# The first mixer's output product as seven half-size products, with the memory's norm and transposes moved to that mixer's start

## The chip, the cores and the metric

One core of a Trainium2 chip. The time is device microseconds of one execution of the whole program, the median of several; beside it one execution was taken with the hardware profiler.

## The reference

Two residual layers over 512 tokens of width 1024, each with a mixer, a cross-attention into 256 memory tokens and a feed-forward part. What matters here is the mixer of layer 0 and the memory's keys and values:

```python
for layer in range(DEPTH):
    h = rmsnorm(x, g_mix_pre[layer])
    # layer 0: forgetting attention (y_a) and short convolution (y_b)
    y = concatenate([y_a, y_b], axis=-1) @ w_out      # 512x1024 @ 1024x1024
    x = x + rmsnorm(y, g_mix_post[layer])
    h = rmsnorm(x, g_cross_pre[layer])
    m = rmsnorm(mem, g_mem[layer])
    y = memory_cross_attention(h, m, w_q, w_kv, w_o)
    ...
```

In the attention the cumulative log of a forget gate (`cum`, from log_sigmoid and a running sum over the tokens) is added to the scores.

## The kernel before

All products run on TensorE as three products of split operands: an operand is a high part (rounded to the matmul's input type, made on ScalarE) and a low part (what is left, made on VectorE), and high x high, high x low and low x high are added up in PSUM. `split_out` (L527) makes both parts; `split_w` does it for a weight tile of 128x1024 that SP has loaded (`st`): `wh` by ScalarE, `wl` by VectorE. PSUM has two families of banks, `bA` and `bB`, taken in turn by `bankA()` and `bankB()`.

Layer 0's mixer is `fox`. It makes v for the attention, the forget gate, then q and k of head pairs 0 and 1 (`qk_pairs(0)`), and then `weave` runs two generators against each other on TensorE: `main` (the convolution's and attention's projections, `conv(0)`, `qk_pairs(2)`, `conv(2)`, then the first column half of the output product) and `side` (the attention of the four head pairs). The forget gate's chain is: `z`, `log1p` (a row of dependent instructions of 8x512 on VectorE), a scan over the tokens, a DMA from GpSimd that writes the sums to `cum`, and a broadcast of `cum` back as `cb` for the first softmax steps (the custom instruction on L1386).

The output product is an `OutProj`: `half0_steps` computes columns 0 to 511 for four row tiles over 8 contraction tiles (in steps of `main`, as operands come), `half1` columns 512 to 1023 row tile by row tile. Each row tile's end is followed by `chain` (sum of squares, gain, addition to x), `next` (the norm of the following sub-layer, `h`) and `transpose` (h into `hT`, through PSUM). That makes 8 x 4 x 2 x 3 = 192 matmuls of 128x512.

The memory is loaded, normalised (`memory_rows`: two squares, a small rstd chain with the power on GpSimd, two scalings, for each of two row tiles) and transposed (`memory_T`) inside `half1` of layer 0. The transposed rows are kept in DRAM as `memT` for layer 1. Then `memory_kv` computes the keys (four chunks c of 48 matmuls of 128x256) and the values (matmuls of 128x512).

Every engine works its queue in order, and what the order is comes from the order in which the program issues, except where a hand-written order holds. SP issues weight loads; after the first loads `pace` puts DRAM copies of the feed-forward's factors behind some of them (`copies`), and `spend` issues accumulating DMAs on GpSimd (`adds`) that make sums of them.

Of the kernel before, what the change touches and what calls it, by code (L numbers as in the profile page):

```python
# [15 lines left out]
P = 128  # L16
# [26 lines left out]
def trunk_kernel(ctx: ExitStack, tc: tile.TileContext, a: dict, out: bass.AP):  # L43
# [103 lines left out]
    def spend(n, behind=None):  # L147
# [16 lines left out]
        ("gp", a["g_mix_pre"][1].rearrange("(m p) -> m p", p=P)),  # L164
    )
# [153 lines left out]
    def put_T_pair(hT, hss, j, gain):  # L319
# [8 lines left out]
        for k, v in ks:  # L328
            nc.scalar.mul(out=hT.hi[k][:, 0:256], in_=v, mul=ch(gain, k))
        for k, v in ks:  # L330
            nc.vector.scalar_tensor_tensor(out=hT.lo[k][:, 0:256], in0=v, scalar=ch(gain, k), in1=f(hT.hi[k][:, 0:256]),
                                           op0=ALU.mult, op1=ALU.subtract)
# [632 lines left out]


# [18 lines left out]
    def memory_T(layer, bank):  # L985


        raw = f(group("mTr")).rearrange("p a (b c) -> p (a b) c", c=MEM)
        ghi, glo = group("mTh"), group("mTl")
        vhi = ghi.rearrange("p a (b c) -> p (a b) c", c=MEM)  # L990
        vlo = glo.rearrange("p a (b c) -> p (a b) c", c=MEM)
        if layer:
            nc.sync.dma_start(out=raw, in_=memT)
        else:
            mg = memory_rows()

        def turn(t):
            for hf in range(2):
# [5 lines left out]
                nc.scalar.copy(out=raw[:, hf * 4:hf * 4 + 4, t * P:(t + 1) * P], in_=ps.rearrange("p (k c) -> p k c", k=4))  # L1004

# [8 lines left out]
        def last():  # L1014
            turn(1)
            nc.gpsimd.dma_start(out=memT, in_=raw)
            parts(range(KT))

        if layer:
            return vhi, vlo, (lambda: parts(range(4)), lambda: parts(range(4, KT)))  # L1020
        return vhi, vlo, (lambda: turn(0), last)

    def memory_kv(layer, vhi, vlo, between):
# [5 lines left out]
        for c in range(4):  # L1029
            ws = w_chunk(w, c * 256)  # L1030
# [8 lines left out]
        between()  # L1039
        vh, vl = group("vh"), group("vl")  # L1040
        for nh in range(2):
# [10 lines left out]
            for j in range(2):  # L1052
                split_out(banks[j], vh[:, 2 * j + nh, :], vl[:, 2 * j + nh, :])
        return kh, kl, vh, vl
# [149 lines left out]
    def fox(proj):  # L1204
# [125 lines left out]
        y = Feat([None] * KT, [None] * KT)  # L1330
        yg, qk, cs = {}, {}, {}
        done = set()
        TO = [(0, 0), (1, 0), (2, 0), (1, 384)]

        def y_group(m):
            if m not in yg:
                yg[m] = group("y")
                y.hi[m], y.lo[m] = yg[m][:, 0, :], yg[m][:, 1, :]
                y.hi[4 + m], y.lo[4 + m] = yg[m][:, 2, :], yg[m][:, 3, :]
            return yg[m]  # L1340
# [237 lines left out]
    for layer in range(2):  # L1578
# [16 lines left out]
        def rest():  # L1595
            for t in (2, 3):
                pm.transpose(t)
# [33 lines left out]
```

## Time and profile before

| | |
|---|---|
| time, median of 3 runs | 1390.54 us (1390.12 to 1390.89) |
| the profiled execution's own time | 1390.6 us |
| its span | 1388.8 us |
| mean granted TensorE clock | 0.996 |
| ScalarE busy | 725.3 us, 52% of the span |
| GpSimd busy | 111.7 us, 8% of the span |
| DMA | 233.62 MB moved, mean 168 GB/s |

The page of the profile lists the busy time of each engine, the chain of work that ended last and the costliest groups of instructions. A row of a timeline has the start and the duration in us, the engine, the line, the operation, the tiles that it writes and reads with their size, and in brackets how long the engine was idle before it and who released it. Matmuls overlap, so their pace is read from their starts. A row of the windows has, for a stretch, the length, then the busy us and the number of instructions of PE, PEld, DVE, ACT and POOL, the granted clock, the DMA share and the GB/s.

### The profile page before, as it was taken

To read this page: it belongs to the slowest core of one execution; us is meant where nothing else is said; L and a number is where in the kernel's file an instruction comes from. 1 tells how busy PE (TensorE), PEld (TensorE's weight loads), DVE (VectorE), ACT (ScalarE), POOL (GpSimd) and SP (SyncE) were. 2 spreads that over 40 slices of the span, in tenths; PEclk is the share of its full clock that TensorE was granted. 3 is DMA by queue.
4 is the path that set the end of the run, shared out by engine and by line. 5 is a ranking of instruction groups with operands and counts; after the bars stand their busy time and mean duration, and the time that the engine had idled before them with its cause. 6 is when DMAs were issued, how large, how long until landed. Compare 5 with 4: busy or idle time off the path is not lost.

```text
span 1388.8 us, 21766 instructions
## 1 busy us (share of the span) xinstructions
PE 1375.6 (99%) x8416; PEld 1225.7 (88%) x8416; DVE 1110.5 (80%) x1801; ACT 725.3 (52%) x1187; POOL 111.7 (8%) x161
## 2 busy tenths in 40 slices
PE   8999999999999999999999999999999999999997
PEld 6778788988899999998889888988889999999886
DVE  6876677646589999989898999663568999999987
ACT  4354456434465444456674797453456444445663
POOL 1000002011010101000011000101200011000001
PEclk9999999999999999999999999999999999999999
DMA  6844452667424567566665657256812555666653
GB/s 225 277 156 158 139 178 66 210 158 148 106 92 137 155 158 186 159 231 229 196 220 178 223 169 248 82 185 153 166 61 92 168 152 174 153 176 239 208 188 132
DMA packets 155250, 233.62 MB, mean 168 GB/s; under 512 B 8477, under 2 KB 90497, under 8 KB 153866
## 3 DMA queue, kind: packets, MB, share of 16 engines
q1 hardware_dynamic: 134706, 180.25, 40.1%
q0 software_dynamic: 17072, 46.16, 15.2%
q10 hardware_dynamic: 3368, 5.82, 1.3%
q8 instruction: 66, 1.08, 0.3%
q14 instruction: 38, 0.31, 0.1%
HBM read 219.60 MB, written 58.74 MB: 200 GB/s over the span
## 4 chain that ended last, share of the span: by engine, by line
PE 98%; DMA 1%; issue 1%; DVE 0%; POOL 0%; SPq 0%; ACT 0%; DVEq 0%; POOLq 0%
PE bA L336 14%; PE bA L338 14%; PE bA L337 14%; PE bB L336 6%; PE bB L337 6%; PE bB L338 6%; PE bB L810 3%; PE bB L812 3%; PE bB L811 3%; PE bA L810 2%; PE bA L812 2%; PE bA L811 2%; PE bA L569 2%; PE bA L571 2%; PE bB L571 2%; PE bB L569 2%
## 5 line engine op out<-in xcount | busy, mean ns | idle before, releaser
L546 DVE TENSOR_TENSOR wl<-st,wh 128x1024 fp32r<-128x1024 f32 x108 | 131.2, 1221 | 96.2 <-ACT wh L545 94.9
L545 ACT CAST wh<-st 128x1024 fp32r<-128x1024 f32 x108 | 113.1, 1050 | 119.5 <-PE bA L337 70.2
L336 PE MATMUL bA<-hTh,wh 128*128 128x512 f32 (+1 forms) x448 | 171.4, 383 | 0.2 <-ACT hTh L314 0.2
L337 PE MATMUL bA<-hTl,wh 128*128 128x512 f32 (+1 forms) x448 | 167.8, 375 | 0.3 <-DVE hTl L315 0.3
L338 PE MATMUL bA<-hTh,wl 128*128 128x512 f32 (+1 forms) x448 | 168.1, 375 | 0.0
L437 ACT CAST wg<-wr 128x1024 fp32r<-128x1024 f32 x80 | 83.6, 1045 | 49.1 <-DVE wr L466 38.4
L776 ACT CAST wh<-st 128x1024 fp32r<-128x1024 f32 x76 | 74.9, 985 | 63.6 <-PE bA L812 27.0
L338 PEld LDWEIGHTS bA<-hTh,wl 128*128 128x128 f32 x448 | 84.3, 188 | 15.4
L438 DVE TENSOR_TENSOR wg<-wr,wg 128x1024 fp32r<-128x1024 f32 x80 | 97.1, 1214 | 0.0
L337 PEld LDWEIGHTS bA<-hTl,wh 128*128 128x128 f32 x448 | 84.6, 189 | 14.1 <-DVE hTl L315 0.5
L336 PEld LDWEIGHTS bA<-hTh,wh 128*128 128x128 f32 x448 | 84.5, 189 | 14.0 <-ACT hTh L314 0.5
L781 DVE TENSOR_TENSOR wl<-st,wh 128x1024 fp32r<-128x1024 f32 x76 | 86.1, 1133 | 10.2 <-ACT wh L776 10.2
L437 ACT CAST wh<-tt 128x1024 fp32r<-128x1024 f32 x40 | 42.1, 1053 | 61.4 <-DVE tt L466 61.4
L336 PE MATMUL bA<-hTq,wh 128*128 128x256 f32 x208 | 59.2, 284 | 0.0
L338 PE MATMUL bA<-hTq,wl 128*128 128x256 f32 x208 | 58.8, 283 | 0.0
L337 PE MATMUL bA<-hTq,wh 128*128 128x256 f32 x208 | 58.8, 283 | 0.0
L810 PE MATMUL bB<-wh,ya 128*128 128x512 f32 x148 | 57.6, 389 | 0.0
L811 PE MATMUL bB<-wl,ya 128*128 128x512 f32 x148 | 57.6, 389 | 0.0
L812 PE MATMUL bB<-wh,ya 128*128 128x512 f32 x148 | 57.6, 389 | 0.0
L756 DVE TENSOR_TENSOR ya<-yb,ya 128x512 fp32r<-128x512 f32 x84 | 53.3, 638 | 0.0
L810 PE MATMUL bA<-wh,ya 128*128 128x512 f32 x132 | 51.3, 389 | 0.0
L811 PE MATMUL bA<-wl,ya 128*128 128x512 f32 x132 | 51.3, 389 | 0.0
(375 smaller groups left out, 4428.4 us busy)
## 6 DMA issues: line engine op xcount, KB each, us to landing
wr<-in_w_ffn_gu_dram SPq DMA_DIRECT2D x80, 512.0 KB
st<-t SPq DMA_DIRECT2D x40, 512.0 KB
t<-in_w_ffn_down_dram SPq DMA_DIRECT2D x32, 512.0 KB
st<-in_w_xkv_dram SPq DMA_DIRECT2D x32, 512.0 KB
st<-in_w_ffn_down_dram SPq DMA_DIRECT2D x30, 512.0 KB
st<-in_ab_w_in_dram SPq DMA_DIRECT2D x24, 512.0 KB
y<-yr POOLq DMA_DIRECT2D x18, 512.0 KB, 3.9
t<-in_w_ffn_down_dram POOLq DMA_DIRECT2D x16, 512.0 KB, 8.7
```

The lines of the kernel that those rows point to most:

```text
L336: nc.tensor.matmul(out=ps, lhsT=wh, rhs=xh, start=first, stop=False)
L337: nc.tensor.matmul(out=ps, lhsT=wh, rhs=xl, start=False, stop=False)
L338: nc.tensor.matmul(out=ps, lhsT=wl, rhs=xh, start=False, stop=last)
L437: return (lambda: nc.scalar.copy(out=to[0], in_=src), lambda: nc.vector.tensor_tensor(out=to[1], in0=src, in1=f(to[0]), op=ALU.subtract))
L438: lambda: nc.vector.tensor_tensor(out=to[1], in0=src, in1=f(to[0]), op=ALU.subtract))
L545: nc.scalar.copy(out=hi, in_=src)
L546: nc.vector.tensor_tensor(out=lo, in0=src, in1=f(hi), op=ALU.subtract)
L776: nc.scalar.copy(out=self.wt[s][0], in_=self.st[s])
L781: nc.vector.tensor_tensor(out=lo, in0=self.st[s], in1=f(hi), op=ALU.subtract)
L810: nc.tensor.matmul(out=banks[t], lhsT=yh, rhs=wh[:, jj, :], start=first and jj == 0, stop=False)
L811: nc.tensor.matmul(out=banks[t], lhsT=yh, rhs=wl[:, jj, :], start=False, stop=False)
L812: nc.tensor.matmul(out=banks[t], lhsT=yl, rhs=wh[:, jj, :], start=False, stop=last and jj == n - 1)
```

## The change

The output product of layer 0's mixer becomes a `MixProj`. With the tokens and the features cut in two, and the columns of the weight too, the product is a 2x2 block product. Its eight block products are replaced by seven (Strassen's scheme in Winograd's form), on sums and differences of blocks. Factors `t1` to `t4` are sums of weight blocks, made in DRAM by a copy and an accumulating DMA each half. Factors `n3`, `s2`, `n1` and `n4` are differences of operand blocks, made in place by VectorE and split there. Each product is two pieces j of 12 matmuls of 128x512 with their own weight tile; the results are combined on VectorE (14 instructions of 128x512).

The memory's rows are loaded and normalised right after `qk_pairs(0)`, and transposed in `main` after `conv(0)`. Both layers read the transposed rows back from `memT`. In layer 0 the gain of the next norm is applied at the transposes' end (`put_T_pair`, with the gain from a table of channels), and h is scaled on ScalarE. The steps behind the product (`tail`) run between the chunks of `memory_kv`.

```diff
+    class MixProj(DownProj):
+        PIECES = tuple((n, j) for n in ("a11", "n3") for j in range(2)) + tuple(
+            (n, j) for j in range(2) for n in ("a22", "a12")) + tuple((n, j) for n in ("s2", "n1", "n4") for j in range(2))
+        B = {"a11": "b11", "n3": "t3", "a22": "t4", "a12": "b21", "s2": "t2", "n1": "t1", "n4": "b22"}
+        SUMS = {"n3": ("a21", "a11"), "s2": ("a22", "n3"), "n1": ("a11", "s2"), "n4": ("a12", "s2")}
...
+        def plan(self):
+            for to, frm, add in (("t3", "b12", "b22"), ("t2", "b11", "t3"), ("t4", "b21", "t2"), ("t1", "b11", "b12")):
+                for js in ((0, 2), (2, 4)):
+                    copies.append(lambda to=to, frm=frm, js=js: nc.sync.dma_start(
+                        out=self.rows(to, *js), in_=self.rows(frm, *js)))
+                    adds.append(lambda to=to, add=add, js=js: nc.gpsimd.dma_start(
+                        out=self.rows(to, *js), in_=self.rows(add, *js), accum_op=ALU.add))
...
+        def sub(self, o, js=slice(0, 4)):
+            x_, y_ = self.SUMS[o]
+            nc.vector.tensor_tensor(out=self.operand(o, js), in0=self.operand(x_, js), in1=self.operand(y_, js), op=ALU.subtract)
...
+        def first_pair(self, j):
+            js = slice(2 * j, 2 * j + 2)
+            self.sub("n3", js)
+            self.split("a11", js)
+            self.split("n3", js)
...
+        def piece(self, s):
+            name, j = self.PIECES[s]
+            self.need(s + 2)
...
+            for kk in range(2):
+                k = 2 * j + kk
+                for t in range(2):
+                    ts = slice(t * P, t * P + P)
+                    bk = self.bk[name][t]
+                    nc.tensor.matmul(out=bk, lhsT=hi[:, k, ts], rhs=wh[:, kk, :], start=k == 0, stop=False)
+                    nc.tensor.matmul(out=bk, lhsT=hi[:, k, ts], rhs=wl[:, kk, :], start=False, stop=False)
+                    nc.tensor.matmul(out=bk, lhsT=lo[:, k, ts], rhs=wh[:, kk, :], start=False, stop=k == 3)
+                    yield 1
...
+        def finish(self, ahead):
+            self.run(8, 9)
+            for o in ("n1", "n4"):
+                self.sub(o)
+                self.split(o)
+            self.need(12)
+            for t in two:
+                tt(self.q[t], bk["s2"][t], self.p1[t], ALU.subtract)
+            self.run(10, 11)
+            for t in two:
+                tt(self.v[t], self.v[t], self.q[t], ALU.add)
+                tt(self.c21[t], bk["a22"][t], self.v[t], ALU.subtract)
+                self.square(t, 0, self.c21[t])
+            for t in two:
+                tt(self.p1[t], bk["a12"][t], self.p1[t], ALU.add)
+                self.square(2 + t, 0, self.p1[t])
+            ws = ahead()
+            for t in two:
+                tt(self.q[t], bk["n1"][t], self.q[t], ALU.add)
+                tt(self.v[t], bk["n1"][t], self.v[t], ALU.add)
+                self.square(t, 1, self.v[t])
+            self.run(12, 13)
+            return ws
...
             def put_b(banks):
                 for i in range(2):
-                    c = cs[m0 + i]
-                    nc.vector.tensor_tensor(out=c, in0=c, in1=banks[i], op=ALU.mult)
-                    gy = y_group(m0 + i)
-                    split_out(c, gy[:, 2, :], gy[:, 3, :])
+                    nc.vector.tensor_tensor(out=proj.act(0, m0 + i), in0=cs[m0 + i], in1=banks[i], op=ALU.mult)
+                proj.first_pair(m0 // 2)
...
         def main():
             yield from conv(0)
+            yield from memory_turn(mg, bankA)
             yield from qk_pairs(2)
             yield from conv(2)
-            yield from proj.half0_steps((4, 6), True, False)
+            yield from proj.piece(0)
+            yield from proj.piece(1)
+            proj.keep("a11")
+            yield from proj.piece(2)
+            yield from proj.piece(3)
+            proj.keep("n3")
             yield lambda: ("y", 1) in done
-            yield from proj.half0_steps((0,), False, False)
+            for m in range(2):
+                proj.split2(m)
+            yield from proj.piece(4)
+            yield from proj.piece(5)
...
         for _ in qk_pairs(0):
             pass
-        proj.y = y
+        mg = memory_rows()
         weave(main(), side())
```

Where the rows stand now is decided by the order of issue. On VectorE around the forget gate's scan, there stood before (`e`, `t` and `z` are the gate's tiles, `qk` a split of q or k):

```order
L188 SCALAR_TENSOR_TENSOR e<-e,t_456 8x512
L1323 MEMSET t_455 8x512
L1320 SCALAR_TENSOR_TENSOR z<-z,e 8x512
L546 TENSOR_TENSOR wl<-st,wh 128x1024
L1324 SCALAR_TENSOR_TENSOR e<-t_455,z 8x512
L546 TENSOR_TENSOR qk<-bA,qk 128x512
L546 TENSOR_TENSOR wl<-st,wh 128x1024
```

And now on VectorE at the same place, where `mem` is the memory's rows (128x512) or their small row statistics (128x1):

```order
L225 TENSOR_SCALAR mem<-mem 128x1
L185 SCALAR_TENSOR_TENSOR e<-e,t_460 8x512
L229 SCALAR_TENSOR_TENSOR mem<-mem 128x1
L185 SCALAR_TENSOR_TENSOR e<-e,t_460 8x512
L1158 TENSOR_SCALAR mem<-mem 128x512
L189 SCALAR_TENSOR_TENSOR e<-e,t_461 8x512
L1497 MEMSET t_460 8x512
L1494 SCALAR_TENSOR_TENSOR z<-z,e 8x512
L1158 TENSOR_SCALAR mem<-mem 128x512
L1498 SCALAR_TENSOR_TENSOR e<-t_460,z 8x512
L547 TENSOR_TENSOR qk<-bA,qk 128x512
```

Four instructions of the memory's norm stand in the gate's chain ahead of the scan (L1498), and the weight split that stood there comes after it.

On ScalarE at the end of `conv(0)`, there stood before (`y` is a split of the convolution's output, `p` a softmax step, `wh` a weight's high part, `pT` the split of a transposed softmax block):

```order
L1390 ACTIVATE p,fx<-p,fx 128x384 x2
L545 CAST y<-cs 128x512
L1390 ACTIVATE p,fx<-p,fx 128x512 x2
L545 CAST wh<-st 128x1024
L545 CAST y<-cs 128x512
```

And now on ScalarE at the same place (`yp` are the high parts of a11 and n3, `mTr` the transposed memory):

```order
L1560 ACTIVATE p,fx<-p,fx 128x384 x2
L1560 ACTIVATE p,fx<-p,fx 128x512 x2
L546 CAST wh<-st 128x1024
L546 CAST yp<-yr 128x2x256 x2
L1171 COPY mTr<-bA 128x4x128 x4
L546 CAST pT<-bB 128x512 x2
```

The four copies out of the transposes' banks stand behind two casts of the convolution's operands.

On VectorE in `memory_kv`, there stood before, for the key chunks:

```order
L631 TENSOR_TENSOR yb<-bB,gain 128x512
L634 SCALAR_TENSOR_TENSOR x_113<-ya,post,x_113 128x512
L634 SCALAR_TENSOR_TENSOR x_113<-yb,post,x_113 128x512
L224 TENSOR_SCALAR pre<-pre 128x1
L228 SCALAR_TENSOR_TENSOR pre<-pre 128x1
L258 SCALAR_TENSOR_TENSOR h<-x_113,pre,gain 128x512 x2
L546 TENSOR_TENSOR wl<-st,wh 128x1024 x2
L546 TENSOR_TENSOR kl<-bA,kh 128x512
```

And now on VectorE, from the last two combinations of the product (L1110) to just behind the first weight split of chunk c = 2 (`c_n` and `c_a` hold results of the product, `kl` the low part of keys):

```order
L1110 TENSOR_TENSOR c_a_1882<-bB,c_a_1882 128x512 x2
L547 TENSOR_TENSOR kl<-bA,kh 128x512
L822 TENSOR_TENSOR c_n_1952<-c_n_1952,gain 128x512 x2
L225 TENSOR_SCALAR post<-post 128x1
L822 TENSOR_TENSOR c_n_1952<-c_n_1952,gain 128x512
L229 SCALAR_TENSOR_TENSOR post<-post 128x1
L822 TENSOR_TENSOR c_n_1952<-c_n_1952,gain 128x512
L831 SCALAR_TENSOR_TENSOR x_110<-c_n_1952,post,x_110 128x512 x2
L225 TENSOR_SCALAR post<-post 128x1
L547 TENSOR_TENSOR wl<-st,wh 128x1024
L229 SCALAR_TENSOR_TENSOR post<-post 128x1
L547 TENSOR_TENSOR kl<-bA,kh 128x512
```

The gain products and additions to x, which stood ahead of the keys, now stand between their weight splits.

200 lines of the change are left out of this document (154 added, 46 removed).

## The prediction

> **What bounds the kernel now.** I read the page's busy times first, then its chain of waits, then TensorE's timeline and the windows around the places that the change touches.
>
> ```profile
> span 1388.8 us, 21766 instructions
> PE 1375.6 (99%) x8416; PEld 1225.7 (88%) x8416; DVE 1110.5 (80%) x1801; ACT 725.3 (52%) x1187; POOL 111.7 (8%) x161
> PE 98%; DMA 1%; issue 1%; DVE 0%; POOL 0%; SPq 0%; ACT 0%; DVEq 0%; POOLq 0%
> ```
>
> TensorE (PE) is busy for 99% of the span and carries 98% of the chain that ended last. So a matmul that is removed counts in full, and so does every pause that is put between two matmuls. The next view is the windows of the stretches that the change touches (busy us and instructions of each engine, granted clock, DMA share, GB/s).
>
> ```profile
> 40.00:60.00 20.00, 20.00 (x90) 16.09 (x89) 19.12 (x41) 6.99 (x9) 0.00 (x0) 1.00 0.98 329
> 60.00:61.00 1.00, 1.00 (x6) 0.82 (x5) 1.00 (x2) 0.00 (x0) 0.00 (x0) 1.00 1.05 403
> 62.00:63.00 1.00, 1.00 (x6) 0.84 (x5) 1.00 (x2) 0.00 (x0) 0.00 (x0) 1.00 0.28 53
> 201.00:258.00 57.00, 57.00 (x362) 51.50 (x361) 38.47 (x72) 32.46 (x69) 7.31 (x12) 1.00 0.39 120
> ```
>
> TensorE has no pause in any of them. But two neighbours are full where the change puts work: VectorE (DVE) is busy 19.12 of 20 us from 40 to 60 us, and the DMA engines 0.98 of it. From 201 to 258 us, mixer's end and memory keys, VectorE has 18.5 us free of 57.
>
> **The saving.** Start to start, from TensorE's timeline, since matmuls overlap and their durations (0.39 us) say nothing of their pace:
>
> ```profile
> 109.81 0.39 PE L336 MATMUL bA<-hTh,wh 128*128 128x512 f32 x1
> ...
> 111.62 0.39 PE L338 MATMUL bA<-hTh,wl 128*128 128x512 f32 x1
> ...
> 234.21 0.28 PE L336 MATMUL bA<-mTh,wh 128*128 128x256 f32 x1
> 234.32 0.28 PE L337 MATMUL bA<-mTl,wh 128*128 128x256 f32 x1
> ...
> 224.10 1.04 PE L305 MATMUL bA<-ident,h 128*128 128x128 f32 x8
> 224.90 0.47 PE L569 MATMUL bB<-rh,y 128*128 128x512 f32 x1
> ```
>
> The first two rows stand eight matmuls apart: 1.81 / 8 = 0.226 us for 128x512. A 128x256 takes about 0.12 (0.11 here), a 128x128 transpose 0.80 / 8 = 0.10. The output product falls from 192 matmuls of 128x512 (8 contraction tiles, 4 row tiles, 2 column halves, 3 split terms) to 7 x 24 = 168. The transposes stay at 16 of the memory and 32 of h. So 24 x 0.226 = **5.4 us** go from TensorE, and nothing else does.
>
> **The first wait: the memory's norm lands in the forget gate's chain.** The chain is VectorE's log1p and scan, a DMA of the sums (cum) to memory, its broadcast back (cb), and the first softmax step of attention(0).
>
> ```profile
> 61.57 1.21 DVE L1324 TENSOR_TENSOR_SCAN e<-t,z 8x512 f32<-8x512 f32 x1
> ...
> 72.31 0.29 DVE L1386 CUSTOM_DVE_ANT_0 p<-bB,cb 128x128 f32<-128x128 f32 x1 [5.70 <-DMA cb<-cum]
> ```
> ```profile
> 63.08 0.71 POOL L1328 DMA_DIRECT2D cum<-e  x1 [36.94 <-DVE e L1324]
> 66.99 1.13 POOL L1364 DMA_DIRECT2D cb<-cum  x2 [3.21 <-DMA cum<-e]
> ```
> ```profile
> 73.01 1.10 PE L1379 MATMUL bB<-qk 64*128 64x384 f32 x6
> ```
>
> Scan end 62.8, cum issued 63.1, cb issued 67.0, first step 72.31. The third group of score matmuls at 73.01 takes a bank which that step frees; the step with its row sum ends at 72.6, so the slack is 0.4 us. The change puts four small instructions and four scalings of the memory's norm around the scan, half of them ahead of it. They wait for four squares on ScalarE (ACT), and these for the memory's rows, which SP issues here:
>
> ```profile
> 51.62 0.56 SPq L694 DMA_DIRECT2D t<-in_w_ffn_down_dram  x1
> 56.56 0.38 SPq L119 DMA_DIRECT2D st<-in_ab_w_in_dram  x1
> 56.99 0.56 SPq L694 DMA_DIRECT2D t<-in_w_ffn_down_dram  x1
> ```
>
> The four loads stand between the first two rows' places. Traffic queued then stays dense until 61 and thins out between 61 and 63 (windows above), so what is issued near 56.9 lands near 62 to 63. The memory's 1 MB at 329 GB/s is 3.2 us more, less 1.6 us for two gain broadcasts of 0.25 MB that go. I take 60 to 62.5 for the four rows. A square takes 0.74 us start to start:
>
> ```profile
> 206.86 0.60 ACT L220 ACTIVATE junk<-bA 128x512 bf16<-128x512 f32 x1 [2.30 <-PE bA L571]
> ...
> 207.60 0.60 ACT L220 ACTIVATE junk<-bA 128x512 bf16<-128x512 f32 x1
> ```
> ```profile
> 213.01 0.88 DVE L982 TENSOR_SCALAR mem<-mem 128x512 f32<-128x512 f32 x2 [0.75 <-POOL mem L232]
> ```
>
> Two squares end near 62, the small steps and the power on GpSimd (0.75 of waiting, row above) near 63; then one scaling (0.42), the last log1p step, the memset and z (0.7 + 0.4 + 0.6), another scaling, and the scan of 1.2: its end near 66.7 in place of 62.8. Less 0.4 of slack, **+3.5 us**. Ends: rows landing 1.5 us earlier give 2; rows at 63.6 give 5.
>
> **Clock.** A pause of that length touches TensorE's clock, as the start shows (windows of 3.41 us):
>
> ```profile
> 6.87:10.28 3.41, 1.48 (x9) 0.84 (x8) 1.26 (x3) 1.37 (x2) 0.00 (x0) 1.00 1.02 402
> 10.28:13.69 3.41, 3.20 (x8) 2.44 (x9) 3.13 (x8) 2.78 (x6) 0.00 (x1) 0.50 1.05 404
> 13.69:17.10 3.41, 2.75 (x15) 1.89 (x14) 2.46 (x3) 0.83 (x2) 1.47 (x1) 1.00 1.08 353
> ```
>
> After a window with 1.48 us of PE work the next was granted 0.50; after one of 3.20 it was 1.00 again. A window at half clock full of matmuls loses 3.41 / 2 = 1.7 us. Pauses of 3.5 and 2.3 us can each leave a window with less than 1.5 us of work, if they fall well. I take **+1.5 us**; ends 0 and 3.4. The Trainium skill ("TensorE: Matmul & The Clock Gate", What's actually happening) has the clock halve after an idle window of about 3.4 us; by that rule neither pause fills a whole window except by luck and the term is nearly nothing. The trace disagrees as far as 1.48 busy of 3.41 was enough, so my term goes by the rows.
>
> **The second wait: memory transposes after conv(0).** They take four bA banks, and ScalarE's copies out of them stand behind two new casts of the convolution's operands. The second cast waits for VectorE's n3 subtraction, and this stands behind a weight split:
>
> ```profile
> 109.83 1.05 ACT L545 CAST wh<-st 128x1024 fp32r<-128x1024 f32 x1
> ...
> 214.99 1.07 ACT L1004 COPY mTr<-bA 128x512 f32<-128x512 f32 x2
> ```
> ```profile
> 111.21 1.22 DVE L546 TENSOR_TENSOR wl<-st,wh 128x1024 fp32r<-128x1024 f32 x1
> 112.35 0.68 DVE L546 TENSOR_TENSOR y<-cs,y 128x512 fp32r<-128x512 f32 x1
> ```
>
> Split end 112.35; subtraction of 128x512 to 112.95; cast to 113.5; copy (0.53) to 114.1. TensorE would be at qk_pairs(2), whose first matmul takes the first of these banks, after 16 transposes from 109.81, at 111.6 to 111.8. **+2.3 us**; ends 1.7 (casts earlier by one VectorE step) and 2.6.
>
> **The third and fourth.** Before the a22 piece ScalarE copies n3's bank out (0.5) and then casts the operand (0.6), while TensorE has the other bank's three matmuls (0.7) to do: with the handovers **+0.7**, ends 0 and 1. Then the stretch from the a22 piece to the first v matmul. TensorE has 120 matmuls of 0.226, 192 of 0.12 and 16 transposes: 27.1 + 23.0 + 1.7 = 52 us. VectorE must do in the same stretch, in this order and all of it needed by its end, 22 operations of 128x1024 (16 weight splits, 3 operand splits, 3 subtractions), 29 of 128x512 (14 combinations, 8 gain products, 7 splits), 8 additions to x, 16 of 128x256 and 14 tiny ones. The paces, start to start:
>
> ```profile
> 241.84 2.35 DVE L546 TENSOR_TENSOR wl<-st,wh 128x1024 fp32r<-128x1024 f32 x2
> 244.11 0.68 DVE L546 TENSOR_TENSOR kl<-bA,kh 128x512 fp32r<-128x512 f32 x1
> ...
> 207.58 0.69 DVE L592 TENSOR_TENSOR ya<-bA,gain 128x512 f32<-128x512 f32 x1 [1.77 <-ACT junk L220]
> 208.19 0.14 DVE L224 TENSOR_SCALAR post<-post 128x1 f32<-128x1 f32 x1
> ...
> 216.56 0.75 DVE L634 SCALAR_TENSOR_TENSOR x<-ya,post,x 128x512 f32<-128x512 f32 x1
> 217.23 0.75 DVE L634 SCALAR_TENSOR_TENSOR x<-yb,post,x 128x512 f32<-128x512 f32 x1
> 223.63 3.25 DVE L1010 SCALAR_TENSOR_TENSOR mTl<-mTr,chan,mTh 128x256 fp32r<-128x256 f32 x8
> 226.80 0.68 DVE L315 TENSOR_TENSOR hTl<-bA,hTh 128x512 fp32r<-128x512 f32 x1
> ```
>
> So 22 x 1.135 + 29 x 0.61 + 8 x 0.67 + 16 x 0.40 + 14 x 0.13 = 56.3 us, and about 1 us in which VectorE waits for ScalarE's first casts: 5 us over. It shows where memory_kv's weight splits come late (c = 2, both halves) and at the first split for v. **+5.0 us**; a pace 5% faster, or idle time that I don't see, gives 2 or 8. ScalarE's gain: eight h scalings leave VectorE, in the sum already.
>
> The weight copies and accumulating sums of the half-size factors (8 and 8 of 512 KB, on SP and GpSimd) go ahead of the FFN's and fall mostly here:
>
> ```profile
> 110.00:190.00 80.00, 80.00 (x421) 63.64 (x421) 54.06 (x121) 40.48 (x79) 1.30 (x4) 1.00 0.45 141
> ```
>
> Over half the DMA time is free there, and 16 transfers of 0.5 MB, read and written at 329 GB/s, take 50 us of it at most in place of the FFN's, which move back: I cost them at nothing, and 3 us each if one came late. The weight load behind the memory's rows on SP lands some 3 us later, but its cast stands behind the first softmax step (72.31): nothing. The memory's transposes read back cost layer 0 a load of 1 MB, some 3 us, with 10 us of pieces ahead of its use: nothing.
>
> **Sum**, against the profiled execution's own 1390.6 us (span 1388.8 and 1.8 around it; the median of the runs shown is 1390.54, so no correction): 1390.6 - 5.4 + 3.5 + 1.5 + 2.3 + 0.7 + 5.0 = **1398.2 us**, 0.55% slower. With the ends: 1390.6 - 5.4 + 2 + 0 + 1.7 + 0 + 2 = 1390.9, and 1390.6 - 5.4 + 5 + 3.4 + 2.6 + 1 + 8 = 1405.2.
>
> **Rivals.**
> - Lead covers the waits. If every operand is ready early enough that lateness is eaten by its lead, only the saving is left: 1390.6 - 5.4 = **1385.2**. It decides where leads exceed 3.5 us at the first softmax step, 2.3 at the memory's banks and 5 in the keys. For it: TensorE paused nowhere between 17 and 742 us before, and 18.5 us of VectorE are free from 201 to 258. Against it: the 0.4 us between step and score matmuls, and that the banks' copies cannot start before the transposes.
> - VectorE fits, the early waits stay: the net addition to VectorE, about 10 us by the instructions, is put into its 18.5 free us. Then 1398.2 - 5.0 = 1393.2; with the memory's rows 1.5 us earlier and no slow window, 1390.2: **no change**. For it: free time is there on average. Against it: weight splits of the pieces move behind the attention's end, seven more than before.
> - The clock halves after each pause: four pauses of 1 to 3 us in the keys leave slow windows too, 3 x 1.7 us on top: **1403**.
>
> **How the numbers follow.** A measurement of this kernel tells about 0.2% (2.8 us) from no change. My forecast has 0.52 (1393.4 to 1401), the lead 0.18, the fit 0.17, the clock 0.13. So slower 0.65, same 0.17, faster 0.18. The range that holds 8 in 10 goes from 1386.5 to 1405.2: it takes in the fit, the clock and both ends of the terms, and leaves out most of the lead.
>
> **What would show it.** TensorE pausing before the third score group of attention(0), with cb the releaser; before qk_pairs(2), with ScalarE's copy of mTr; in memory_kv before a matmul with wl, VectorE the releaser and busy throughout. 168 matmuls in the pieces at 0.226 show the saving. Slow windows show in the granted clock behind 73 and 112 us. The forecast is wrong if the memory's rows land before 57 us, or if VectorE shows idle time between the a22 piece and v.

## The result, and the profile after

| | before | after |
|---|---|---|
| time, median of 4 runs each | 1390.33 us (1390.01 to 1390.89) | 1407.15 us (1403.35 to 1409.81) |
| the profiled execution's own time | 1390.6 us | 1409.81 us |
| matmuls in the records | 8416 | 8392 |
| mean granted TensorE clock | 0.996 | 0.990 |

The change is slower: the ratio is 1.0118, its interval 1.0092 to 1.0145. The forecast was 1398.2 with a range of 1386.5 to 1405.2. The sign was right, and the loss was more than twice what was forecast: 16.8 us between the medians in place of 7.6.

The page of after: the span, the busy time of each engine, and the chain by engines.

```profile
span 1407.9 us, 21840 instructions
PE 1380.5 (98%) x8392; PEld 1227.9 (87%) x8392; DVE 1129.1 (80%) x1829; ACT 743.0 (53%) x1216; POOL 131.2 (9%) x173
PE 91%; DVE 3%; DMA 2%; issue 1%; ACT 1%; POOL 1%; SPq 0%; DVEq 0%; POOLq 0%; ACTq 0%
```

The matmuls fell by 24, exactly as the change says. Yet TensorE's busy time rose by 4.9 us in a span that is 19.1 longer: it does less work, some of it at a lower clock, and it pauses. The chain says who it waits for: VectorE, DMA, ScalarE and GpSimd hold 7% of it, against 1% before. The windows of after (length; busy us and instructions of PE, PEld, DVE, ACT, POOL; granted clock; DMA share; GB/s) show where:

```profile
72.40:75.82 3.42, 1.18 (x6) 0.61 (x4) 0.63 (x3) 0.07 (x1) 0.00 (x0) 1.00 0.82 179
75.82:79.23 3.41, 2.51 (x9) 1.67 (x10) 1.56 (x7) 1.86 (x5) 0.00 (x0) 0.50 0.79 286
79.23:82.64 3.41, 3.41 (x9) 2.32 (x7) 3.05 (x13) 1.66 (x6) 0.00 (x0) 0.50 0.40 108
116.77:120.19 3.42, 1.16 (x11) 0.91 (x10) 3.28 (x5) 2.10 (x5) 0.00 (x0) 1.00 0.21 40
120.19:123.60 3.41, 3.41 (x11) 2.73 (x12) 0.55 (x2) 1.86 (x4) 0.54 (x1) 0.50 0.99 378
249.90:253.31 3.41, 1.17 (x10) 0.96 (x9) 2.95 (x7) 1.59 (x5) 0.88 (x1) 1.00 0.00 0
253.31:256.72 3.41, 2.72 (x12) 2.64 (x12) 2.92 (x6) 2.38 (x7) 0.55 (x1) 0.50 0.39 124
256.72:260.14 3.42, 2.65 (x12) 2.44 (x12) 3.42 (x9) 0.71 (x2) 1.62 (x1) 0.50 0.45 120
260.14:263.55 3.41, 3.41 (x18) 3.41 (x17) 2.57 (x5) 0.52 (x1) 3.37 (x2) 0.50 0.44 138
270.38:273.79 3.41, 2.50 (x20) 2.18 (x19) 3.41 (x9) 3.38 (x9) 0.00 (x0) 1.00 0.00 0
273.79:277.20 3.41, 1.94 (x8) 1.61 (x9) 3.41 (x9) 2.06 (x5) 1.25 (x1) 1.00 0.19 50
201.00:258.00 57.00, 51.93 (x276) 44.53 (x275) 48.55 (x69) 38.26 (x65) 1.43 (x2) 0.96 0.68 238
210.44:272.49 62.05, 57.18 (x329) 51.19 (x329) 53.33 (x83) 41.91 (x76) 7.48 (x6) 0.92 0.58 200
```

From 201 to 258 us TensorE was busy throughout before; now it is idle for 5.1 us. The short windows are cut where the granted clock changes, which is at steps of 3.41 us. Three of them, at 72, 117 and 250 us, hold 1.2 us of work, and behind each the clock is 0.50: for two windows, one, and three. It stays at 0.50 as long as a slow window has pauses of its own (2.51, 2.72 and 2.65 us busy), and is back behind a full one. Together 20.5 us were at half clock between 20 and 1376 us; before, none of that stretch was. The last pause, at 272.5, falls on two windows (2.50 and 1.94 busy) and slows nothing.

The pauses themselves, from TensorE's timeline of after: the first and second wait.

```profile
73.13 0.40 PE L339 MATMUL bA<-hTh,wl 128*128 128x512 f32 x1
75.77 0.66 PE L1549 MATMUL bB<-qk 64*128 64x384 f32 x1 [2.24 <-DVE fx L1556]
77.33 1.32 PE L1549 MATMUL bB<-qk 64*128 64x384 f32 x5 [0.90 <-DVE fx L1556]
```
```profile
115.88 1.91 PE L1168 MATMUL bA<-ident,mem 128*128 128x128 f32 x16
120.05 0.69 PE L337 MATMUL bA<-hTh,wh 128*128 128x512 f32 x1 [2.26 <-ACT mTr L1171]
```

And three of those in memory_kv:

```profile
239.30 0.39 PE L339 MATMUL bA<-mTh,wl 128*128 128x256 f32 x1 [0.85 <-DVE wl L547]
254.00 0.58 PE L339 MATMUL bA<-mTh,wl 128*128 128x256 f32 x1 [2.93 <-DVE wl L547]
275.26 0.50 PE L1222 MATMUL bA<-wl,mTh 128*128 128x512 f32 x1 [2.38 <-DVE wl L547]
```

Counted as time between two starts beyond their usual spacing, the first wait is 2.4 + 1.4 = 3.8 us and the second 2.4. In the same way the a22 piece pauses 0.7 us at 209.5, and memory_kv 1.0 (at 238), 3.1 (251), 1.1 (256.5), 0.5 (264.5) and 2.5 (272.5), together 8.2.

### The profile page after: what moved, and what is told of

Same layout as the page of the kernel before. It is cut to its first block, busy times and chain, and to the rows that moved or that the text cites. A ratio compares the mean times of both kernels' runs of the same rounds, so it can differ in the third digit from the quotient of the medians.

```text
span 1407.9 us, 21840 instructions
## 1 busy us (share of the span) xinstructions
PE 1380.5 (98%) x8392; PEld 1227.9 (87%) x8392; DVE 1129.1 (80%) x1829; ACT 743.0 (53%) x1216; POOL 131.2 (9%) x173
## 4 chain that ended last, share of the span: by engine, by line
PE 91%; DVE 3%; DMA 2%; issue 1%; ACT 1%; POOL 1%; SPq 0%; DVEq 0%; POOLq 0%; ACTq 0%
PE bA L337 13%; PE bA L339 13%; PE bA L338 13%; PE bB L337 6%; PE bB L338 6%; PE bB L339 6%; PE bB L813 3%; PE bB L811 3%; PE bB L812 3%; PE bA L813 2%; PE bA L811 2%; PE bA L812 2%; PE bA L572 2%; PE bA L570 2%; PE bA L571 2%; PE bA L1405 1%
## 5 line engine op out<-in xcount | busy, mean ns | idle before, releaser
L547 DVE TENSOR_TENSOR wl<-st,wh 128x1024 fp32r<-128x1024 f32 x118 | 142.9, 1222 | 89.7 <-ACT wh L546 88.8
L546 ACT CAST wh<-st 128x1024 fp32r<-128x1024 f32 x118 | 123.8, 1052 | 107.3 <-PE bA L338 59.6
L777 ACT CAST wh<-st 128x1024 fp32r<-128x1024 f32 x76 | 75.0, 987 | 62.2 <-PE bA L813 26.9
L782 DVE TENSOR_TENSOR wl<-st,wh 128x1024 fp32r<-128x1024 f32 x76 | 86.7, 1141 | 10.1 <-ACT wh L777 10.1
L233 POOL TENSOR_TENSOR post<-post,nhalf 128x1 f32<-128x1 f32 x24 | 15.1, 632 | 500.4 <-DVE post L229 500.4
```

The source lines that it names most:

```text
L546: nc.scalar.copy(out=hi, in_=src)
L547: nc.vector.tensor_tensor(out=lo, in0=src, in1=f(hi), op=ALU.subtract)
L777: nc.scalar.copy(out=self.wt[s][0], in_=self.st[s])
L782: nc.vector.tensor_tensor(out=lo, in0=self.st[s], in1=f(hi), op=ALU.subtract)
```

## The experiments

Where nothing else is said, an experiment is the changed kernel with the edit shown, timed against the kernel before, whose median was 1390.3 to 1391.2 us each time. "Below the change" is against the change's median of 1407.15.

### The memory's rows and their norm behind conv(0)'s first products

```diff
+                else:
+                    rows.append(memory_rows())
...
-            yield from memory_turn(mg, bankA)
+            yield from memory_turn(rows[0], bankA)
...
-        mg = memory_rows()
         weave(main(), side())
```

> The change, with the memory's rows loaded and normalised after the first convolution projection instead of ahead of the attention, so that nothing of the norm stands around the gate's scan. Theory A (the norm's instructions on VectorE wait for late rows and hold up the scan, and the pause halves the clock): no pause over 0.5 us before the third score group of attention(0), no half-clock window near 75 us, the excess of TensorE between 72 and 85 us falls from 5.7 us to under 0.7, the time is about 5 us below the change. Rival (cb is late because the queues carry more traffic): the scan ends early but cb still lands after 75 us, and 2 us or more of the pause stay.

1403.97 us (1402.4 to 1408.64), ratio 1.010 [1.008, 1.012]. The scan is back at 61.5, and the first softmax step at 72.08. But the pause stays, and the timeline of this kernel shows why:

```profile
67.02 3.09 SPq L1152 DMA_DIRECT2D mem<-in_mem_dram  x4
72.08 0.29 DVE L1556 CUSTOM_DVE_ANT_0 p<-bB,cb 128x128 f32<-128x128 f32 x1 [5.52 <-DMA cb<-cum]
75.81 0.29 DVE L1556 CUSTOM_DVE_ANT_0 p<-bB,cb 128x128 f32<-128x128 f32 x1 [3.43 <-DMA cb<-cum]
```

SP now issues the memory's four loads from 67 us on, while the broadcast cb is under way, and the second cb lands at 75.8. The edit moved two things, the arithmetic and the transfers, and put a collision of transfers in the place of the wait. It answers nothing on the norm alone; the next one does.

### Only the norm's arithmetic there; the loads stay

```diff
-    def memory_rows():
+    def memory_load():
...
+        return mg
+
+    def memory_norm(mg):
...
+                else:
+                    memory_norm(mg)
...
-        mg = memory_rows()
+        mg = memory_load()
```

> The change with the memory's rows loaded where the change loads them, and only squares, rstd and scalings moved behind the first convolution projection. Theory A, mended by the run in which the loads moved too (there the 1 MB of loads ran into the broadcast of the sums): now neither the scan nor the broadcast is held up, no pause over 0.5 us near 73 us, the excess from 72 to 85 us under 0.7, no half-clock window there, 4 to 5.5 us below the change. Rival (the loads themselves, wherever they stand, make the broadcast late): 2 us or more of pause stay.

1402.23 us (1401.42 to 1403.02), ratio 1.0078 [1.0064, 1.0092], 4.9 below the change. The steps of the two softmax rows, and the two windows of the second wait, of this kernel:

```profile
72.31 0.29 DVE L1561 CUSTOM_DVE_ANT_0 p<-bB,cb 128x128 f32<-128x128 f32 x1 [5.64 <-DMA cb<-cum]
72.93 0.29 DVE L1561 CUSTOM_DVE_ANT_0 p<-bB,cb 128x128 f32<-128x128 f32 x1 [0.33 <-DMA cb<-cum]
```
```profile
110.12:113.53 3.41, 1.57 (x15) 1.32 (x13) 3.27 (x6) 2.04 (x4) 0.00 (x0) 1.00 0.19 41
113.53:116.95 3.42, 2.99 (x18) 2.50 (x18) 1.30 (x2) 2.42 (x5) 0.54 (x1) 1.00 0.93 338
```

The first pause and its two slow windows are gone: the norm's place in VectorE's queue was the cause. The windows show something on the clock: the second wait is still there, as long as in the change (2.4 us), but it falls on two windows here, with 1.57 and 2.99 us of work, and the clock stays full. In the change it fell on one and cost a slow window.

### The memory's copies ahead of the operand casts

```diff
-                proj.first_pair(m0 // 2)
+                if m0:
+                    proj.first_pair(m0 // 2)
...
             yield from memory_turn(mg, bankA)
+            proj.first_pair(0)
```

> The change, with the first operand splits issued after the memory's transposes, so that ScalarE's copies out of the transposes' banks stand ahead of its two casts. Theory A: the pause of 2.5 us before qk_pairs(2) falls under 0.5 and the slow window behind it goes, about 4 us less than the change. Rival (what TensorE waits for there is VectorE's or the weights' work, and the copies only end last by chance): the pause moves to another releaser and less than 1 us is won.

1403.31 us (1402.17 to 1405.18), ratio 1.0091 [1.0076, 1.0106], 3.8 below the change. In the timeline of this kernel qk_pairs(2) follows the transposes at once:

```profile
114.52 1.91 PE L1168 MATMUL bA<-ident,mem 128*128 128x128 f32 x16
116.19 0.47 PE L337 MATMUL bA<-hTh,wh 128*128 128x512 f32 x1
```

The pause of 2.4 and its slow window at 120 are gone. The first wait (3.8 us) and the pauses before wl (2.8 and 1.1) stay. The rest of memory_kv came out differently, though the edit does not touch it: no pause at 238 or before the split for v, and 3.0 us at h's transposes in place of 0.5. So the second wait is shown: ScalarE's copies stood behind the two casts.

### A VectorE step that waits for the powers, ahead of the gain products

```diff
                 for t in two:
                     self.next_raw(t)
-                for t in two:
-                    self.gain(0, self.p1[t])
-                    self.gain(1, self.q[t])
+                fz = nc.vector.tensor_tensor(out=stats("fz")[:, 0:1], in0=self.r[0], in1=self.r[1], op=ALU.add).ins
+                with tc.issue_after(fz):
+                    for t in two:
+                        self.gain(0, self.p1[t])
+                        self.gain(1, self.q[t])
```

The reason for it lies in the timeline of after, where memory_kv pauses. GpSimd makes the powers (pre) of h's norm; ScalarE's scalings of h wait for them; behind these stand the casts kh and wh; and VectorE waits for kh.

```profile
258.43 1.89 DVE L822 TENSOR_TENSOR c_a<-c_a,gain 128x512 f32<-128x512 f32 x3
258.52 4.99 POOL L233 TENSOR_TENSOR pre<-pre,nhalf 128x1 f32<-128x1 f32 x2 [3.46 <-DVE pre L229]
260.24 2.35 DVE L547 TENSOR_TENSOR wl<-st,wh 128x1024 fp32r<-128x1024 f32 x2
263.03 2.57 ACT L847 ACTIVATE h<-x,pre 128x512 f32<-128x512 f32 x4 [5.60 <-POOL pre L233]
266.44 0.57 ACT L546 CAST kh<-bA 128x512 fp32r<-128x512 f32 x1
267.05 0.69 DVE L547 TENSOR_TENSOR kl<-bA,kh 128x512 fp32r<-128x512 f32 x1 [4.33 <-ACT kh L546]
```

Two numbers for each of 128 partitions took 4.99 us here. Before, each took 0.55 in this part (timeline of before):

```profile
234.60 0.55 POOL L232 TENSOR_TENSOR pre<-pre,nhalf 128x1 f32<-128x1 f32 x1 [3.06 <-DVE pre L228]
```

> The change, with one tiny VectorE instruction that reads the power results of x0 and x1, ahead of the four gain products behind it, so that VectorE pauses for GpSimd there. Theory A (GpSimd's power of 128x1 is held off while VectorE works through instructions with two operands in SBUF): the pair of powers falls from 5.0 to under 2.5 us, h starts 1.5 us or more earlier against the row statistics, the pause before the first low-part matmul of v falls from 2.5 to under 1.5 us. Rival (GpSimd is late for a reason of its own, a queue or the DMAs that it issues): the pair still takes 4 us or more, and the time is the change's or 1 us worse.

1403.15 us (1401.34 to 1405.07), ratio 1.0093 [1.0076, 1.011], 4.0 below the change. The pair now:

```profile
255.93 2.05 POOL L233 TENSOR_TENSOR pre<-pre,nhalf 128x1 f32<-128x1 f32 x2 [3.99 <-DVE pre L229]
```

The pauses at h's transposes (0.5) and before the split for v (2.5) are gone; those of 3.1 and 1.1 (1.5 here) stay, since they lie ahead of this step, the fence. Not all of the 4.0 is the fence's: the pause of 1.0 at 238 is gone too, and the first wait is 3.0 us with one slow window in place of 3.8 with two, and both lie ahead of the fence. So one of memory_kv's mechanisms is GpSimd's power beside VectorE's products.

### What holds a power: four tests behind the kernel's end

Each test starts two powers of 128x1 in a row when a small VectorE step is done, while VectorE goes on with one kind of work. A first version showed nothing: its powers all came out ahead of the work that should have run beside them, one every 0.52 us. What it expected:

> The change with five small groups behind its end: each a tiny VectorE instruction, then none, or six additions of 128x1024 with two SBUF operands, or twelve of 128x512 with one operand in PSUM, or ten scalings of 128x1024 with one SBUF operand, or none, and two GpSimd powers of 128x1 that wait only for the tiny instruction. Theory A: about 0.55 us each beside no work; with two SBUF operands the powers end only near the end of the six additions (some 6 us); beside PSUM operands 0.6 to 1 us. Rival: 0.55 us in every group. The time is some 20 us longer than the change's and says nothing else.

The second version chains each power behind an instruction of its own group:

```diff
+    def probe(op, n):
+        st = stats("probe")
+        op(1)
+        nc.vector.tensor_scalar(out=st[:, 3:4], in0=x[2][:, 0:1], scalar1=0.0, scalar2=2.0, op0=ALU.mult, op1=ALU.add)
+        op(n)
+        for c in (4, 5):
+            nc.gpsimd.tensor_tensor(out=st[:, c:c + 1], in0=st[:, 3:4], in1=nhalf, op=ALU.pow)
...
+    for op, n in ((none, 0), (two_sbuf, 5), (psum_sbuf, 10), (one_sbuf, 10), (none, 0)):
+        probe(op, n)
```

> The change with five small groups behind its end, on data that no output reads. In each a tiny VectorE instruction releases two GpSimd powers of 128x1, while VectorE goes on with nothing, five additions of 128x1024 with two SBUF operands, ten of 128x512 with one operand in PSUM and one in SBUF, ten scalings of 128x1024 with one SBUF operand, nothing. Theory A: 0.52 to 0.55 us a power beside nothing; beside two SBUF operands the powers end only near the end of the five additions (5.7 us of them); beside a PSUM operand 0.6 to 1 us. The rival: 0.55 us everywhere. The time means nothing here.

GpSimd's timeline of this test, the first four groups in order (the fifth, beside nothing again, took 1.06 us like the first):

```profile
1399.90 1.06 POOL L1818 TENSOR_TENSOR probe<-probe,nhalf 128x1 f32<-128x1 f32 x2 [2.17 <-DVE probe L1815]
1402.75 2.85 POOL L1818 TENSOR_TENSOR probe<-probe,nhalf 128x1 f32<-128x1 f32 x2 [1.79 <-DVE probe L1815]
1410.30 1.06 POOL L1818 TENSOR_TENSOR probe<-probe,nhalf 128x1 f32<-128x1 f32 x2 [4.70 <-DVE probe L1815]
1418.86 2.08 POOL L1818 TENSOR_TENSOR probe<-probe,nhalf 128x1 f32<-128x1 f32 x2 [7.50 <-DVE probe L1815]
```

Beside nothing, and beside additions with an operand in PSUM, a pair takes 1.06 us. Beside additions of two operands in SBUF (where all tiles lie that are not in PSUM) it takes 2.85, beside scalings of one SBUF operand 2.08. The Trainium skill ("SBUF — State Buffer", 🔬 SBUF: two separate sides) has VectorE and GpSimd share a port pair there, held for a whole instruction by whoever starts first; these rows agree. Neither the theory (some 5.7 us beside the additions) nor the rival (0.55 a power everywhere) came out: the longest power took 1.6 us, while one addition ran, and not the 4.5 of the kernel. Two more tests, with the same chaining, changed the work beside the pair: chained and independent additions of 128x512,

> As the earlier probe, with two other groups between the empty ones: ten additions of 128x512 with two SBUF operands all into one tile (each waits for the one before), and ten into four tiles in turn (free to follow back to back). Theory A (GpSimd gets in only between VectorE instructions that leave a gap): beside the chained ones a power starts within one addition, a pair in under 2.5 us; beside the free ones the pair ends only near the end of the ten (5 to 6 us). Rival (a power waits for one or two running instructions in both): the same 2 to 2.5 us in both.

and weight splits and products in place like the kernel's.

> The kernel with a test behind its end: pairs of powers on GpSimd (128x1, as the norm's) that start when a small VectorE step is done, beside (1) nothing, (2) four weight splits of 128x1024 with fp32r output, two tiles in turn, (3) four gain products of 128x512 in place and then two such splits, as in the keys, (4) nothing. Adds held a power for one instruction only. Theory: what held one power for 4.5 us in the kernel is in the kind of instruction, the split with its rounded output or the product in place; then the first power beside (2) lasts 3.5 to 4.9 us, or beside (3) 3.5 to 5 us, and ends 0.3 to 0.5 us after the last of them. Rival: each kind holds for one instruction only; then the first power lasts at most 1.7 us in (2) and 1.1 us in (3), and what held it in the kernel is elsewhere, as in the transfers that ran there. (1) and (4): 1.06 a pair.

Ten additions one behind the other: 1.78 us a pair; ten independent ones, back to back: 1.53; four splits: 2.72; four products and two splits: 1.53. In each of them a power waited for one VectorE instruction and was done before the next one ended. So neither the lack of a gap nor the kind of instruction alone holds it for longer; the theories of both tests fell. The four splits had gaps of 0.03 us between them, where the kernel's have none; but the first two rows below show splits without a gap that let a power in after one. What does hold it is open. That it happens, and not always, the kernels themselves show, with the same order on VectorE (two small steps, then three splits), first without the fence and second with it (a later pair of powers, which the fence does not touch). The experiment with the copies first:

```profile
270.23 3.49 DVE L547 TENSOR_TENSOR wl<-st,wh 128x1024 fp32r<-128x1024 f32 x3
270.32 2.67 POOL L233 TENSOR_TENSOR pre<-pre,nhalf 128x1 f32<-128x1 f32 x2 [7.99 <-DVE pre L229]
```

The experiment with the fence:

```profile
270.98 3.49 DVE L547 TENSOR_TENSOR wl<-st,wh 128x1024 fp32r<-128x1024 f32 x3
271.07 4.32 POOL L233 TENSOR_TENSOR pre<-pre,nhalf 128x1 f32<-128x1 f32 x2 [7.00 <-DVE pre L229]
```

The pair got in between two splits in the one, and had to wait until all three were done in the other.

### The steps behind the product spread over more chunks

```diff
+            elif c == 1:
                 for t in two:
...
+            elif c == 2:
+                for t in two:
                     self.add(t, (self.c21[t], self.v[t]))
-            elif c == 1:
+            elif c == 3:
                 for t in two:
                     self.next_raw(t)
+                self.fence(0, 1)
...
+            elif c == 4:
+                self.pairs(0)
+            elif c == 5:
...
+                between({(0, 2): 4, (0, 4): 5, (1, 2): 7}.get((nh, k2)))
```

> The change with only the steps behind the product spread further over keys and values (and a VectorE pause at each power whose reader is ScalarE); the first two pauses and that before the a22 piece stay as they are. Theory A: from the a22 piece to the first v matmul 51 to 53 us in place of 62, no half-clock window there, pauses of the change near 73, 112 and 205 us unchanged, so 10 to 11 us below the change: 1395 to 1399. Rival (the keys were only helped by the lead that the earlier edits gave): 57 us or more for the stretch, 1400 and above.

1397.41 us (1393.21 to 1398.68), ratio 1.0047 [1.0032, 1.0062], 9.7 below the change. The two early waits are still there (2.8 and 2.4 us, a slow window behind each), but in memory_kv only pauses of 0.9 and 1.2 us are left of 8.2, and no slow window. So the pauses before wl at 251 and 256.5 came of VectorE's order: products, small steps and additions to x in a row, ahead of splits that TensorE needed sooner. There was room for both, once they were spread.

### All of it

The norm's arithmetic late, the copies first, the steps spread with the fence, and the a22 operand split ahead of the copy of n3:

```diff
             yield from proj.piece(3)
-            proj.keep("n3")
             yield lambda: ("y", 1) in done
             for m in range(2):
                 proj.split2(m)
+            proj.keep("n3")
```

> The change with the norm's arithmetic late, the transposes' copies ahead of the operand splits, the a22 operands cast ahead of the copy of n3, and the steps behind the product spread further over keys and values, so that gain products and additions of rows 2 and 3 come in the values, with a VectorE pause at each power whose reader is ScalarE. Theory A (the saving of 5.4 us is there, and the four waits with their slow clock are all that is lost): pauses of under 1 us each, no half-clock window between 20 and 1380 us, 1386 to 1390 us, below the kernel before. Rival (the added VectorE work must be paid somewhere): the pauses move on into values or queries and the time stays above 1395.

1386.30 us (1385.29 to 1386.8), ratio 0.9965 [0.9951, 0.9979]: it beats both kernels. The busy times of its page, and the window from the a22 piece to the first v matmul:

```profile
PE 1369.1 (99%) x8392; PEld 1219.4 (88%) x8392; DVE 1127.9 (82%) x1831; ACT 739.3 (53%) x1216; POOL 125.4 (9%) x173
```
```profile
199.25:249.49 50.24, 50.24 (x314) 45.56 (x313) 47.80 (x69) 34.80 (x59) 4.42 (x4) 1.00 0.76 252
```

VectorE does as much as in the change (1127.9 of 1129.1 us), ScalarE too. TensorE has no pause over 0.3 us from 20 to 736 and no slow window, and TensorE carries 98% of the chain, as before. The time below before is 4.9 us: the 24 matmuls saved.

### The same without spreading the steps

The norm late, the copies first, the a22 operand first and the fence; the steps behind the product in the change's chunks.

> As the run with all edits, but with the steps behind the product in the change's places, and only the fence of VectorE behind the powers of x0 and x1. Theory A: no pauses near 73, 112 and 205 us; in the keys the weight splits still come late, 1 + 3 + 1.5 us, with one or two half-clock windows: 1394 to 1398 us. Rival (an engine that has more lead at the keys' start loses less there): under 2 us of pause in the keys and 1389 to 1392.

1390.21 us (1388.83 to 1391.1), ratio 0.9992 [0.9983, 1.0001]: no difference from before that this can tell. The theory (1394 to 1398, with the splits late) fell, and the rival's time came. The pauses before wl are gone here without spreading. Two things differ from the change. VectorE ends the first split of the keys 2.5 us before TensorE needs it, where the change ended it 1.0 us late. And its order is another: two weight splits stand ahead of the second pair of additions to x, where the change has one. What is left in memory_kv are 0.5 and 2.1 us at h's transposes (ScalarE's h, with its casts between) and one slow window. So the pauses before wl came not of too much work for VectorE, but of its order together with a late start. Spreading alone removes them, and so do the other edits without spreading; which part the earlier start has in that, and which the changed order, this run does not separate.

## Why the prediction was right in its sign and wrong in its size

| term of the sum | forecast | measured in the profiled execution |
|---|---|---|
| 24 matmuls | -5.4 | -24 in the records; 1386.30 against 1391.23 once no wait is left: -4.9 |
| first wait, forget gate | +3.5 | +3.8 |
| clock | +1.5 | +7.8 |
| second wait, the memory's copies | +2.3 | +2.4 |
| a22 operand | +0.7 | +0.7 |
| memory_kv | +5.0 | +8.2 |
| not foreseen: a pause at 1056 us | | +1.0 |

From 1390.6 us the measured column (with -5.4) comes to 1409.1, against 1409.8 for that execution. The clock's 7.8 is what is left when all pauses (16.1) are taken off the 23.9 us that TensorE's starts lie further apart, in all, than before; 20.5 us at half clock can cost at most 10.2. Counted in the same way, the slow windows of the experiments cost 8.1 us where there are six, 5.4 and 5.1 where there are four, 3.8 for three, 2.9 for two and 1.6 for one. With these and its pauses, of over 0.35 us, 1390.6 - 5.4 comes to within 1.1 us of the profiled execution of each of the seven timed experiments, so nothing larger is missing from the account. The pause at 1056 was not followed up. The median lies 2.7 below the profiled execution; the other runs had mean clocks of 0.991, 0.993 and 0.994.

**The saving** holds.

**The first wait** went as worked out, in VectorE's own order (timelines of after):

```profile
61.19 0.63 ACT L221 ACTIVATE junk<-mem 128x512 bf16<-128x512 f32 x1 [6.38 <-DMA mem<-in_mem_dram]
61.95 0.15 DVE L225 TENSOR_SCALAR mem<-mem 128x1 f32<-128x1 f32 x1 [4.23 <-ACT junk L221]
66.38 1.20 DVE L1498 TENSOR_TENSOR_SCAN e<-t,z 8x512 f32<-8x512 f32 x1
75.42 0.29 DVE L1556 CUSTOM_DVE_ANT_0 p<-bB,cb 128x128 f32<-128x128 f32 x1 [2.68 <-DMA cb<-cum]
```

The rows landed at 61.2, inside the 60 to 62.5 that was taken; the scan ended at 67.6, against 66.7. The norm's arithmetic moved away removes the wait, as shown. **The second wait and the a22 operand** are right to 0.1 us, and the experiments with the copies first, and with all of it, remove both.

**The clock is the step that failed most.** The prediction said: "Pauses of 3.5 and 2.3 us can each leave a window with less than 1.5 us of work, if they fall well. I take **+1.5 us**; ends 0 and 3.4." The limit was about right: windows with 1.2 us of work were all followed by a slow one. What failed is the count. It gave the two early waits less than one slow window (1.7 us) between them, as if it took luck. But of a pause of 2.4 us, 1.9 or more lie in one window unless a border falls between 0.5 and 1.9 us into it, and that has a chance of 1.4 in 3.41. In this execution both pauses lay mostly in one window. Then the first wait, which comes in two parts, kept the clock down for a second window; and the pauses of memory_kv, for which the sum had no clock at all, brought three in a row. Six slow windows, at most 1.7 us each, are the 7.8. The rival "the clock halves after each pause" was nearest in kind and gave 1403; it counted one window for a pause, and did not see that the next pause keeps the clock from coming back. The luck is there too, but in the size: where the pauses fall on the windows differs between executions, and the times of the same kernel go from 1403.35 to 1409.81.

**memory_kv was put on the wrong cause.** "TensorE 52 us, VectorE 56.3" and "about 1 us in which VectorE waits". TensorE's part was right: 62.05 us less 9.7 of pauses and clock is 52.3. But VectorE was busy for 53.3 us (56.3 was forecast; the terms given there add up to 56.2) and idle for 8.7. The view of waits, VectorE in that stretch (us in total, times, longest), says for what:

```profile
DVE kl L547 <- ACT kh L546: 5.7, 2, 4.3
DVE yl L547 <- ACT yh L546: 1.7, 2, 1.4
DVE wl L547 <- ACT wh L546: 1.3, 2, 1.1
DVE x L831 <- POOL post L233: 1.1, 3, 0.5
```

By work alone VectorE would have been 1 us late. It was late by its order and by a loop through three engines: VectorE's products hold GpSimd's power, the power holds ScalarE's h, h holds kh, and kh holds VectorE. The prediction named this as the sign against itself, "if VectorE shows idle time between the a22 piece and v", and the idle time is there. The rival "VectorE fits" was right on the work and wrong on what follows from it; the version with everything spread is where it comes true.

**Costed at nothing** were the 16 transfers of the half-size factors, the weight load behind the memory's rows and the transposes read back. One transfer did come late, and it makes the pause at 238. A cast on ScalarE waited for its weight tile (timeline of after):

```profile
225.44 1.06 ACT L546 CAST wh<-st 128x1024 fp32r<-128x1024 f32 x1 [2.40 <-DMA st<-in_ab_w_out_dram]
```

VectorE lost 1.05 us at 226.5 behind this cast, was busy without a break from there to the keys' first split, and that came 1.0 us late. Where the tile came in time (the experiments with rows and norm moved, with the copies first and with the fence) VectorE lost 0.3 us there and the pause is gone; where VectorE lost 0.6 (only the arithmetic moved) and 0.9 (the steps spread), the pause is 0.6 and 0.9. So 1.0 of memory_kv's 8.2 is a transfer that was priced at nothing; what held it up was not followed up. Loads also collide where they meet a broadcast on the path: that is the experiment which moved the memory's loads.

**The range** was too narrow at its upper end because the terms' ends left out that they share a cause: each pause that comes true can also cost clock.

## What to carry to other kernels

On a full TensorE, price a pause of 2 us or more together with a slow window of up to 1.7 us behind it (two of the pauses here fell on two windows and cost none), and a row of pauses a few us apart with one for each 3.41 us until they end. A sum of work against work says only whether things can fit; whether they do is set by the order in each queue, so follow one result through all the engines that it passes (here VectorE, GpSimd, ScalarE and back) and ask who stands ahead of it in each. When part of a change is moved, move its arithmetic and its transfers one at a time: each alone can undo the gain of the other.

## What the runs showed of the hardware

- A power of 128x1 on GpSimd took 0.55 us alone, 1.6 beside one VectorE addition of 128x1024 with both operands in SBUF, no more than alone beside additions with an operand in PSUM, and up to 4.5 in the kernel while VectorE ran five instructions of SBUF operands one behind the other. Why it is at times let in after one instruction and at times only after all is open.
- Windows of 3.41 us that had full clock and 1.25 us of TensorE's work or less were followed by half clock in every case looked at; those with 1.94 or more kept it. Between the two both happened: 1.57 kept it (rows above), and 1.54 (254.24 to 257.66 us, the experiment with the copies first), 1.85 (73.71 to 77.12, the steps spread) and 1.92 (73.88 to 77.29, the fence) did not. So the profile's busy time is not quite what the clock goes by. From half clock 2.72 us of busy time did not bring it back (row above); 2.91 did (247.42 to 250.83, the copies first). The Trainium skill ("TensorE: Matmul & The Clock Gate", What's actually happening) asks for an idle window; by these rows a window that is two thirds idle (1.16 to 1.18 us busy of 3.41) is enough.
